# Attention scores on TensorE: the low parts of the keys as 64-row matmuls, two heads in different row groups

## The chip, the cores and the metric

One Trainium2 chip, of which the kernel uses one core. The metric is the device time of one execution in microseconds. Before the change three executions took 2203.68, 2203.01 and 2199.96 us, with a median of 2203.01 us.

## The reference, cut to what matters

The reference is one layer of a hybrid encoder block on 512 frames of width 2048: RMSNorm, one wide input projection, sixteen heads of banded softmax attention beside four heads of gated linear attention, an output projection, a gated MLP with a short convolution, a per-layer embedding gate, and a last norm. The change lies in the attention scores:

```python
def one_chunk(args):
    c, qc = args
    start = c * CHUNK
    kb = lax.dynamic_slice_in_dim(k_pad, start, band, axis=1)
    vb = lax.dynamic_slice_in_dim(v_pad, start, band, axis=1)
    s = jnp.einsum('bqhd,bkhd->bhqk', qc, kb).astype(jnp.float32) * scale + bias
    valid = (start + key_off) >= 0
    s = jnp.where(valid[None, None, None, :], s, neg)
    pr = jax.nn.softmax(s, axis=-1).astype(vb.dtype)
    return jnp.einsum('bhqk,bkhd->bqhd', pr, vb)
```

The head dimension is 64. All operands are float32.

## The kernel before, in words

Nearly all the work is on TensorE (PE). Each float32 operand of a large matmul is split into a high part, which is the value rounded to the faster matmul type fp32r, and a low part, the remainder. A product is then three matmuls: high by high, high by low, low by high. The weights are split while the kernel runs: ScalarE (ACT) writes the high part of a weight page and VectorE (DVE) subtracts it to get the low part (tile `w`). The large projections use seven products in place of eight (operands named `R11`, `N1`, `T3` and so on), and one product of one output block is one step: 24 matmuls of 128x128 by 128x256 into one of the PSUM banks `accA`, `accB`, `accC`. ACT and DVE collect the banks into a page `u`.

The order of the work is written out by hand. The main loop goes through the steps, and an `agenda` tells for each step which further pieces are issued before or after its product. A helper class (line 64, under which nearly every instruction is recorded) keeps the instructions of PE, ACT and DVE in program order.

The attention belongs to eight units of the first stage, one unit for two heads (s = 0 and 1). `attend` hangs its pieces on the agenda, from two to thirteen steps behind the unit's start. `high` and `low` make the operands from `u`, whose partitions 0 to 63 hold head 0 and 64 to 127 hold head 1:

- `Q` of a head holds the high part of its 64 query rows in the head's own half of the partitions, and the low part in the other half.
- `Kh` holds the keys' high part in both halves, and `Kl` the keys' low part in both halves.

A matmul of all 128 rows of `Q` with `Kh` is therefore (query high + query low) by key high, and one with `Kl` is (query high + query low) by key low. `scores(h)` issues both into the PSUM tile `psc` of a head, of which there are four rotating banks for `psc` and for the transposed probabilities `ptr`. `TILES` puts the four query tiles into three parts, h = 0, 1 and 2, with rows of 512, of 384, and twice of 256 key columns. `scores` of one unit is thus 16 matmuls, 8 of them with `Kl`. One step later `soft` on DVE reads `psc` (output `sc` or `scb`), ACT takes the exponential, PE turns the result (`ptr`), ACT evicts it (`PT`), and `values` multiplies with `V` (output `py`). The matmuls of `py` have 64 output columns, and the two heads write to different halves of the PSUM partitions.

Of the kernel before, what the change touches and what calls it, by code (L numbers as in the profile page):

```python
# [8 lines left out]
F32 = mybir.dt.float32  # L9
# [3 lines left out]
ALU = mybir.AluOpType  # L13

P = 128
# [27 lines left out]
def encoder_block(ctx: ExitStack, tc: tile.TileContext, A, out):  # L43
# [26 lines left out]
    vec, act, ten = InOrder(nc.vector), InOrder(nc.scalar), InOrder(nc.tensor)  # L70
# [49 lines left out]
    def psum_aux(name):  # L120
        return aux[0](name)
# [648 lines left out]
    TILES = ((3,), (2,), (1, 0))  # L770
# [3 lines left out]
    def attend(unit):  # L774
        b, M = unit.u, {}
        o = unit.o
# [25 lines left out]
        def low():  # L802
            for s in range(2):
                a, z = slice(s * 64, s * 64 + 64), slice(64 - s * 64, 128 - s * 64)
                vec.scalar_tensor_tensor(M["Q", s][z], o[a, 0, :], 0.125, M["Q", s][a].bitcast(F32), ALU.mult, ALU.subtract)
                for r in (a, z):
                    vec.tensor_tensor(M["Kl", s][r], o[a, 1, :], M["Kh", s][a].bitcast(F32), ALU.subtract)

        def scores(h):
            for s in range(2):  # L810
                psc = M["psc", s, h] = psum_aux("psc")
                for i, qt in enumerate(TILES[h]):
                    w = slice(256 * i, 256 * i + max(P * (qt + 1), 256))
                    nn = w.stop - w.start
                    ql = M["Q", s][:, qt * P:(qt + 1) * P]
                    ten.matmul(psc[:, w], ql, M["Kh", s][:, :nn], start=True, stop=False)
                    ten.matmul(psc[:, w], ql, M["Kl", s][:, :nn], start=False, stop=True)

        def soft(h):
            t, at = (tile_("scb", 768) if h == 1 else tile_("sc", 1024)), 0  # L820
# [43 lines left out]
        def result():  # L864
            if b % 2 == 0:
                ypair[:] = [page("c", "yp").rearrange("p (s t) -> p s t", s=2)]
            act.activation(ypair[0][:, b % 2, :], M["y"], AF.Copy)

        items = [(2, 7, load_e if b else lambda: None), (2, 2, high), (3, 1, low), (4, 1, mask), (5, 0, load_v), (11, 1, result)]
        if b % 2:  # L870
            items.append((12, 1, lambda: store_pair(mixd, b // 2, ypair[0][:, 0, :], ypair[0][:, 1, :])))
        for h in range(3):
            items += [(t + h, k, lambda f=f, h=h: f(h)) for t, k, f in (
                (5, 6, scores), (6, 1, soft), (7, 1, normal), (7, 5, turn), (8, 1, evict), (8 + (h == 1), 4, values))]
# [75 lines left out]
    for a, b in zip(stages[2:], stages[3:]):  # L950
        i0 = base[a.units[-1]]
        for n, p in enumerate(PLAIN):
            op = PRODUCTS[p][1]
            for g in range(2):
                start = 2 * n + 2 + g
                if g and b.chained:
                    start = max(start, 5)
# [878 lines left out]
```

## Time and profile before

| | |
|---|---|
| median of three executions | 2203.01 us |
| span of the profiled execution | 6266.3 us |
| matmuls in it | 18248 |
| PE busy | 6253.6 us (100%) |
| DVE busy | 1910.0 us (30%) |
| ACT busy | 1349.7 us (22%) |

The profiled execution is 2.84 times as long as the median of the executions without a profile. The two kinds of time are therefore kept apart below: "profiled" and "unprofiled". The profile has no record of the granted clock (its column PEclk shows 1.00 throughout). The profiled execution's own time is its span, 6266.3 us; what lies around it was not recorded.

How to read it: a row of grouped instructions gives the engine, the operation, output<-inputs, the shape, the count after x, then the busy time in us and the mean duration of one in ns, and after the last bar the idle time of the engine before them with what ended it. PE's matmul rows overlap one another, so the busy time over the count, not the mean, is the distance from one to the next. The chain of waits is followed back from the last instruction.

### The profile page before, as it was taken

Reading aid. Unit: us, or ns where it says so; the run is one execution under the profiler, and the core shown is the slowest. Engines: PE = TensorE matmul, PEld = TensorE weight load, DVE = VectorE, ACT = ScalarE, POOL = GpSimd, SP = SyncE. Lnnn points to the kernel's source line nnn. Section 1 sums busy time; section 2 is a strip of 40 time slices with the busy share of each in tenths; the row PEclk is TensorE's granted clock in tenths of the full one; section 3 lists DMA queues with packets and bytes.
Section 4 is the critical chain, followed back from the end, with each engine's and each line's share of the span. In section 5 each row is a group of like instructions: output and inputs, shape, how many; then the busy total and the mean of one; then the engine's idle time right before and its main releaser. Section 6 shows DMA issues by size and latency. Waiting matters only on the chain.

```text
span 6266.3 us, 45637 instructions
## 1 busy us (share of the span) xinstructions
PE 6253.6 (100%) x18248; PEld 5819.7 (93%) x18248; DVE 1910.0 (30%) x2585; ACT 1349.7 (22%) x1960; POOL 215.6 (3%) x261
## 2 busy tenths in 40 slices
PE   9999999999999999999999999999999999999999
PEld 5555999988989799999999999999999999999999
DVE  2222222222222233333333333333333232233333
ACT  2111111222221222222222222222222121222322
POOL 0000000000000000000000000000000000000000
DMA  1123222222222334344444443333333242333432
GB/s 67 34 81 64 61 71 57 72 74 63 70 70 87 110 100 122 101 108 116 113 113 103 112 107 92 83 78 87 79 108 95 61 113 70 109 101 114 121 110 88
DMA packets 200037, 561.39 MB, mean 90 GB/s; under 512 B 21808, under 2 KB 64048, under 8 KB 199824
## 3 DMA queue, kind: packets, MB, share of 16 engines
q1 hardware_dynamic: 163184, 431.28, 21.0%
q0 software_dynamic: 34656, 124.27, 11.5%
q8 instruction: 143, 2.34, 0.2%
q10 hardware_dynamic: 1984, 2.92, 0.1%
q14 instruction: 70, 0.57, 0.0%
HBM read 484.99 MB, written 119.54 MB: 96 GB/s over the span
## 4 chain that ended last, share of the span: by engine, by line
PE 100%; DVE 0%; issue 0%; DVEq 0%; ACT 0%; POOL 0%; POOLq 0%
PE accA L64 48%; PE accC L64 24%; PE accB L64 12%; PE v L64 5%; PE vaA L64 2%; PE vaC L64 1%; PE pp L64 1%; PE psc L64 1%; PE ptr L64 1%; PE py L64 1%; PE po L64 1%; PE vaD L64 1%; PE vaB L64 1%; PE plr L64 0%; PE pu L64 0%; PE pat L64 0%
## 5 line engine op out<-in xcount | busy, mean ns | idle before, releaser
L64 PE MATMUL accA<-h,w 128*128 128x256 f32 x5088 | 1695.5, 563 | 0.0
L64 PEld LDWEIGHTS accA<-h,w 128*128 128x128 f32 x5088 | 1673.7, 473 | 13.1 <-issue 11.6
L64 PE MATMUL accC<-h,w 128*128 128x256 f32 x4248 | 1347.7, 542 | 0.0
L64 PEld LDWEIGHTS accC<-h,w 128*128 128x128 f32 x4248 | 1330.8, 454 | 1.6 <-issue 0.6
L64 DVE TENSOR_TENSOR w<-s,w 128x1024 fp32r<-128x1024 f32 (+1 forms) x381 | 458.4, 1203 | 1100.4 <-ACT w L64 1100.4
L64 DVE TENSOR_TENSOR w<-l,w 128x1024 fp32r<-128x1024 f32 (+1 forms) x320 | 383.2, 1197 | 612.1 <-ACT w L64 607.6
L64 ACT ACTIVATE u<-accA 128x256 f32<-128x256 f32 x302 | 116.1, 384 | 2033.4 <-PE accA L64 2033.4
L64 ACT ACTIVATE w<-l 128x1024 fp32r<-128x1024 f32 (+1 forms) x320 | 331.8, 1037 | 956.1 <-PE accC L64 557.4
L64 ACT ACTIVATE w<-s 128x1024 fp32r<-128x1024 f32 (+1 forms) x381 | 395.0, 1037 | 327.5 <-PE accB L64 203.2
L64 PE MATMUL accA<-up_R,w 128*128 128x256 f32 x1056 | 325.3, 531 | 0.0
L64 PE MATMUL accA<-up_N,w 128*128 128x256 f32 x1056 | 324.2, 530 | 0.0
L64 PE MATMUL accB<-up_R,w 128*128 128x256 f32 x1056 | 323.7, 529 | 0.0
L64 PEld LDWEIGHTS accA<-up_R,w 128*128 128x128 f32 x1056 | 320.5, 441 | 1.6 <-issue 0.8
L64 PEld LDWEIGHTS accA<-up_N,w 128*128 128x128 f32 x1056 | 320.6, 442 | 0.0
L64 PEld LDWEIGHTS accB<-up_R,w 128*128 128x128 f32 x1056 | 320.5, 442 | 0.0
L64 PE MATMUL v<-w,h 128*128 128x512 f32 x384 | 318.6, 1100 | 0.0
L64 PEld LDWEIGHTS v<-w,h 128*128 128x128 f32 x384 | 165.2, 431 | 150.5 <-issue 150.1
L64 DVE TENSOR_TENSOR s<-s,l 128x1024 f32<-128x1024 f32 (+1 forms) x176 | 211.2, 1200 | 0.0
L64 DVE TENSOR_TENSOR u<-u,accC 128x256 f32<-128x256 f32 x102 | 43.0, 421 | 547.7 <-PE accC L64 547.7
L64 DVE TENSOR_TENSOR u<-u,accA 128x256 f32<-128x256 f32 x98 | 41.3, 421 | 510.4 <-PE accA L64 510.4
L64 DVE TENSOR_TENSOR u<-u,accB 128x256 f32<-128x256 f32 x100 | 42.1, 421 | 479.4 <-PE accB L64 479.4
L64 ACT ACTIVATE u<-accC 128x256 f32<-128x256 f32 x98 | 37.7, 384 | 603.5 <-PE accC L64 603.5
(303 smaller groups left out, 5554.9 us busy)
## 6 DMA issues: line engine op xcount, KB each, us to landing
l<-in_w_up SPq DMA_DIRECT2D x132, 512.0 KB, 3.5
s<-in_w_up SPq DMA_DIRECT2D x84, 512.0 KB, 3.5
s<-in_w_up POOLq DMA_DIRECT2D x84, 512.0 KB, 5.5
l<-in_w_dn SPq DMA_DIRECT2D x56, 448.0 KB, 3.4
l<-in_w_blk SPq DMA_DIRECT2D x48, 512.0 KB, 3.5
s<-in_w_blk SPq DMA_DIRECT2D x32, 512.0 KB, 3.5
s<-in_w_blk POOLq DMA_DIRECT2D x32, 512.0 KB, 6.1
l<-in_w_out SPq DMA_DIRECT2D x28, 512.0 KB, 3.6
```

The costliest lines, as they stand in the source:

```text
L64: ins = f(*args, **kw)
```

## The change

`low` writes the keys' low part only in the head's own half of the partitions, which removes one of two DVE instructions per head. `scores` multiplies `Kl` with only the 64 rows that hold the query's high part, so the product of the two low parts falls away. The order is also another one: both heads' PSUM tiles are taken first, and for each query tile there follow `Kh` of head 0, `Kh` of head 1, `Kl` of head 0 (rows 0 to 63), `Kl` of head 1 (rows 64 to 127).

```diff
@@ attend: low, scores
             for s in range(2):
                 a, z = slice(s * 64, s * 64 + 64), slice(64 - s * 64, 128 - s * 64)
                 vec.scalar_tensor_tensor(M["Q", s][z], o[a, 0, :], 0.125, M["Q", s][a].bitcast(F32), ALU.mult, ALU.subtract)
-                for r in (a, z):
-                    vec.tensor_tensor(M["Kl", s][r], o[a, 1, :], M["Kh", s][a].bitcast(F32), ALU.subtract)
+                vec.tensor_tensor(M["Kl", s][a], o[a, 1, :], M["Kh", s][a].bitcast(F32), ALU.subtract)
 
         def scores(h):
             for s in range(2):
-                psc = M["psc", s, h] = psum_aux("psc")
-                for i, qt in enumerate(TILES[h]):
-                    w = slice(256 * i, 256 * i + max(P * (qt + 1), 256))
-                    nn = w.stop - w.start
-                    ql = M["Q", s][:, qt * P:(qt + 1) * P]
-                    ten.matmul(psc[:, w], ql, M["Kh", s][:, :nn], start=True, stop=False)
-                    ten.matmul(psc[:, w], ql, M["Kl", s][:, :nn], start=False, stop=True)
+                M["psc", s, h] = psum_aux("psc")
+            for i, qt in enumerate(TILES[h]):
+                n = max(P * (qt + 1), 256)
+                for name in ("Kh", "Kl"):
+                    for s in range(2):
+                        rows = slice(0, P) if name == "Kh" else slice(s * 64, s * 64 + 64)
+                        ten.matmul(M["psc", s, h][:, 256 * i:256 * i + n], M["Q", s][rows, qt * P:(qt + 1) * P],
+                                   M[name, s][rows, :n], start=name == "Kh", stop=name == "Kl")
```

On TensorE, at the first attention unit and h = 0 and 1 (`_3107` and `_3108` are the high parts of head 0 and head 1, `_3109` and `_3110` the low parts, `_3105` and `_3106` the queries; `accB`, `accA` and `accC` are products of the input projection):

```order
 L64 MATMUL psc<-Kh_3107,Q_3105 128x512
+L64 MATMUL psc<-Kh_3108,Q_3106 128x512
 L64 MATMUL psc<-Kl_3109,Q_3105 128x512
-L64 MATMUL psc<-Kh_3108,Q_3106 128x512
 L64 MATMUL psc<-Kl_3110,Q_3106 128x512
 L64 MATMUL accA<-h_102,w 128x256 x24
 L64 MATMUL psc<-Kh_3107,Q_3105 128x384
+L64 MATMUL psc<-Kh_3108,Q_3106 128x384
 L64 MATMUL psc<-Kl_3109,Q_3105 128x384
-L64 MATMUL psc<-Kh_3108,Q_3106 128x384
 L64 MATMUL psc<-Kl_3110,Q_3106 128x384
```

Head 1's high product moves ahead of head 0's low product, and the two low products stand one behind the other; the number of matmuls is the same, and the shape shown is the output's, so that the 64 rows of the low products can't be seen in it.

On DVE, in `low` of the same unit (`u` is the unit's output, the `w` behind it the low part of a weight page that a coming product needs):

```order
 L64 SCALAR_TENSOR_TENSOR Q_3105<-u,Q_3105 64x512
-L64 TENSOR_TENSOR Kl_3109<-u,Kh_3107 64x512 x2
+L64 TENSOR_TENSOR Kl_3109<-u,Kh_3107 64x512
 L64 SCALAR_TENSOR_TENSOR Q_3106<-u,Q_3106 64x512
-L64 TENSOR_TENSOR Kl_3110<-u,Kh_3108 64x512 x2
+L64 TENSOR_TENSOR Kl_3110<-u,Kh_3108 64x512
 L64 TENSOR_TENSOR w<-l_2938,w 128x1024
```

Two of six instructions are gone ahead of the weight's low part, in each of the eight units; nothing else moves on this engine. ACT and POOL keep their instructions and their order. On SP's DMA queue one store of the attention's result (`mix_R`<-`yp`) stands two places later, behind the loads of a weight page and of a page for the MLP; all else stands as it did.

## The prediction

> **What bounds the kernel now.** I read the page first, then the groups of instructions by form, the busy time by stretches, and at last the order of time around the scores. The page's head, its engines and its chain of waits:
>
> ```profile
> span 6266.3 us, 45637 instructions
> PE 6253.6 (100%) x18248; PEld 5819.7 (93%) x18248; DVE 1910.0 (30%) x2585; ACT 1349.7 (22%) x1960; POOL 215.6 (3%) x261
> PE 100%; DVE 0%; issue 0%; DVEq 0%; ACT 0%; POOL 0%; POOLq 0%
> ```
>
> The reader is to see that in the profiled execution PE is the whole chain: nobody makes it wait. But this execution is 2.84 times as long as the unprofiled median (6266.3 / 2203.01), so the question is what of this picture holds at the true speed. The groups of the attention's stretch (1100 to 1900 us), of a later one (3100 to 4200 us) and of the whole tell which durations change with the stage:
>
> ```profile
> L64 PE MATMUL accC<-in_R,w 128*128 128x256 f32 x216 | 91.8, 689 | 0.0
> ```
>
> ```profile
> L64 DVE TENSOR_TENSOR s<-s,l 128x1024 f32<-128x1024 f32 x18 | 21.9, 1215 | 0.0
> ```
>
> ```profile
> L64 PE MATMUL accC<-h,w 128*128 128x256 f32 x1056 | 324.7, 530 | 0.0
> ```
>
> ```profile
> L64 DVE TENSOR_TENSOR s<-s,l 128x1024 f32<-128x1024 f32 x152 | 185.1, 1218 | 0.0
> ```
>
> In the attention's stretch a 256-column matmul takes 91.8 / 216 = 425 ns, later 324.7 / 1056 = 307 ns; the unprofiled execution has 2203.01 us for 18248 matmuls, 121 ns for each if PE does nothing else. The groups by form show that nearly all of these have 256 columns, so a column costs at most about 0.47 ns unprofiled, against 1.66 profiled here. The DVE instruction of 1024 columns takes 1.22 us there and in the mean of the whole. So PE was slowed in the profile, DVE was not, and unprofiled DVE is a much larger share: 1910.0 of 2203 us, 87%. By stretches:
>
> ```profile
> 1100.00:1900.00 800.00, 800.00 (x2054) 724.34 (x2054) 214.41 (x503) 176.88 (x332) 27.27 (x31) 1.00 0.27 71
> 3100.00:4200.00 1100.00, 1100.00 (x3697) 1100.00 (x3696) 378.79 (x443) 233.91 (x311) 55.91 (x64) 1.00 0.40 99
> ```
>
> (Columns: stretch, length, then busy time and count of PE, weight loads, DVE, ACT, POOL, the clock, and DMA.) In the attention's stretch 800 us of PE shrink to 800 x 0.47 / 1.66 = 227 us, while DVE keeps its 214 us. Unprofiled, the two engines are near balance there; either can be the bound, and that is the heart of this prediction.
>
> **The change, step by step.** First the low products. Their groups, and the first unit's scores in order of time:
>
> ```profile
> L64 PE MATMUL psc<-Kl,Q 128*128 128x256 f32 x32 | 22.1, 691 | 0.0
> ...
> L64 PE MATMUL psc<-Kl,Q 128*128 128x512 f32 x16 | 17.3, 1079 | 0.0
> ...
> L64 PE MATMUL psc<-Kl,Q 128*128 128x384 f32 x16 | 13.7, 859 | 0.0
> ```
>
> ```profile
> 1170.69 1.00 PE L64 MATMUL psc<-Kh,Q 128*128 128x512 f32 x1
> 1171.53 1.00 PE L64 MATMUL psc<-Kl,Q 128*128 128x512 f32 x1
> 1172.21 1.15 PE L64 MATMUL psc<-Kh,Q 128*128 128x512 f32 x1
> 1173.05 1.16 PE L64 MATMUL psc<-Kl,Q 128*128 128x512 f32 x1
> 1173.89 6.46 PE L64 MATMUL accA<-h,w 128*128 128x256 f32 x15
> ```
>
> From start to start a 512-column matmul takes 0.84 us (once 0.68), 1.64 ns a column. The 64 low products stream 32x256 + 16x512 + 16x384 = 22528 columns: 36.9 us profiled. If the two heads' 64-row matmuls run side by side, half goes: 18.5 us profiled, and 22528 x 0.47 / 2 = 5.3 us unprofiled. No row shows two row groups at once. The nearest shows two column groups: `py` ahead of a transpose, both of 128 columns of float32.
>
> ```profile
> 1208.81 3.94 PE L64 MATMUL accA<-h,w 128*128 128x256 f32 x9
> 1212.68 3.43 PE L64 MATMUL py<-PT,va 128*64 128x128 f32 x16
> 1216.04 2.01 PE L64 MATMUL ptr<-ident,scb 128*128 128x128 f32 x5
> ```
>
> Sixteen `py` take 1216.04 - 1212.68 = 3.36 us, 0.21 each, where five `ptr` take about 0.40 each: the halves do run in pairs. I take full overlap from this row; the other end is none, no gain.
>
> The same rows price the switch between matmuls of the whole array and of a part. Nine `accA` should take 9 x 0.42 = 3.78 us and take 3.87: the first `py` comes 0.09 us late. The sixteen `py` take just eight slots of 0.42, so leaving them costs 0 here. The weight loads of the same place show why a switch could cost more:
>
> ```profile
> 1209.23 3.01 PEld L64 LDWEIGHTS accA<-h,w 128*128 128x128 f32 x7
> 1212.68 2.57 PEld L64 LDWEIGHTS py<-PT,va 128*64 128x64 f32 x16 [0.43 <-issue]
> 1216.04 1.73 PEld L64 LDWEIGHTS ptr<-ident,scb 128*128 128x128 f32 x6 [0.79 <-issue]
> ```
>
> In a stream the loads run without a break; at a switch they sit idle for 0.43 or 0.79 us and start only with their own matmul. The change makes 64 switches: each pair of `Kl` is entered and left, 4 pairs in each of 8 units. Bounds: 0, and 64 x 0.09 = 5.8 us, profiled. Unprofiled, if the 0.09 follows the array's speed it is 0.09 x 0.47 / 1.66 = 0.025 us, 1.6 us in all; if it is a fixed delay, 5.8 us. I take the middle, 3.5 us (0.055 a switch).
>
> Here the Trainium skill speaks against the change: "TensorEngine Tiling (Array Packing)", Key Properties, says that a change of the tiling mode, not just of the tile, drains TensorE. The idle weight loads above agree that nothing is loaded ahead. "TensorE: Matmul & The Clock Gate", Single matmul latency, gives a lone warm matmul 398 cycles at 2.4 GHz beyond its columns, an estimated 0.166 us for one drain; 64 of them would be 10.6 us, and the sum below would end at 2206.1 us instead of 2199.0. The row's 0.09 us on the slower array is about half of that, so I weigh it as a rival.
>
> Second, the DVE instructions:
>
> ```profile
> 1141.88 0.69 DVE L64 SCALAR_TENSOR_TENSOR Q<-u,Q 64x512 fp32r<-64x512 f32 x1
> 1142.58 1.38 DVE L64 TENSOR_TENSOR Kl<-u,Kh 64x512 fp32r<-64x512 f32 x2
> 1143.98 0.69 DVE L64 SCALAR_TENSOR_TENSOR Q<-u,Q 64x512 fp32r<-64x512 f32 x1
> 1144.68 1.39 DVE L64 TENSOR_TENSOR Kl<-u,Kh 64x512 fp32r<-64x512 f32 x2
> 1146.10 1.22 DVE L64 TENSOR_TENSOR w<-l,w 128x1024 fp32r<-128x1024 f32 x1
> ```
>
> Two `Kl` take 1.40 us, so one of each two removes 0.70 us, 16 times: 11.2 us of DVE. Profiled this is worth nothing, since PE never waits for DVE; PE's slow stream covers it. Unprofiled the cover is 227 us of PE over 214 us of DVE, and the `w` behind these instructions is what PE's coming product waits for. Bounds: 0 (PE stays the bound) and -11.2 us (DVE is). I take a fifth, 2.2 us: the chain of waits in the attention's stretch shows DVE idle until another engine's work ends, so on these rows it is not yet the bound:
>
> ```profile
> DVE w L64 <- ACT w L64: 148.0, 18, 14.0
> ...
> DVE sc L64 <- PE psc L64: 119.3, 26, 14.1
> ```
>
> Third, the order. Head 0's `psc` is now complete three slots after the start instead of two, head 1's after three instead of four. DVE, which waits for `psc` (the last row), gets head 0 a slot later, at most 512 x 0.47 = 0.24 us, 24 times, if it stands ready; ACT's exponentials queue behind it. This is one reason for a fifth and no more. Head 1's bank must be free one matmul earlier; with four banks in rotation I cost that at nothing, and if it were not, PE's whole queue would stand behind that matmul for up to 0.24 us. The store that SP issues two places later is read only by the next stage: nothing; if that were late, the next stage's first load would be.
>
> The sum, profiled: 6266.3 - 18.5 + 5.8 = 6253.6 us. Unprofiled, against the median: 2203.0 - 5.3 + 3.5 - 2.2 = 2199.0 us, 0.18% less. Changes under about 0.2% (4.4 us) can't be told from none on this kernel, whose three runs lie 0.17% apart.
>
> **The rivals.**
>
> - DVE is the bound in the attention's stretch. For it: 214 of 227 us before any gaps. Against it: the two waits above, which are DVE waiting. Then PE's part is hidden and all of the DVE work counts: 2203.0 - 11.2 = 2191.8 us.
> - The switches are dear, and the kernel is slower. Place: ahead of and behind each pair of `Kl`. On a faster array the weight load at a switch is no longer hidden by the matmul ahead. The shortest load of `py` took 132 ns, so a switch may cost 0.09 + 0.13 = 0.22 us, 64 x 0.22 = 14.1 us: 2203.0 - 5.3 + 14.1 = 2211.8 us, with PE bound and DVE's relief worth nothing. It decides from 5.3 / 64 = 0.08 us a switch, and is over 0.2% from 0.15 us. The skill's drain of 0.166 us would lie there. Against it: `py` is entered 16 times with no more than the 0.09.
>
> ```profile
> L64 PEld LDWEIGHTS py<-PT,va x320: 132/294/294, 1212.7 to 1878.1; 128*64 128x64 f32 x160
> ```
>
> - The row groups don't run side by side, so the change doesn't do what it says: 2203.0 + 3.5 - 2.2 = 2204.3 us. For it: no row shows row groups. Against it: the pairs of `py`.
>
> **How the numbers follow.** My forecast, with pairs side by side, switches of 0.025 to 0.09 us and little from DVE, has 0.49 and runs from 2195 to 2203; I predict its 2199.0. DVE as the bound has 0.19 (2191 to 2195), dear switches 0.16 (2206 to 2212), no overlap 0.16 (2202 to 2207). The range of 2191 to 2208 leaves out the far end of the dear switches and whatever goes beyond the DVE work. Faster by over 0.2%, below 2198.6: a little under half of the forecast and all of the DVE case, 0.41. Slower by over 0.2%, above 2207.4: most of the dear switches and a rest of the third rival, 0.15. Within: 0.44.
>
> **What would show it.** In the profile after, the low products' starts come in pairs, and the second of a pair starts within some hundredths of a us of the first; the scores of h = 0 take about 2.5 us instead of 3.2. The next `accA` starts no more than 0.1 us late. `Kl` on DVE counts 16 instead of 32. The profiled span falls by about 13 us. If it falls so and the unprofiled time doesn't, the cover by DVE or a fixed cost of the switches is the cause. The prediction is wrong if the starts within a pair are a full matmul apart, if weight loads stand idle for much more than the 0.43 us at each switch, or if the unprofiled time falls by more than the 7.5 us that PE's and DVE's shares here make without the switches.

## The result, and the profile after

The changed kernel is slower. Eighteen executions have a median of 2210.13 us (2204.35 to 2213.88), eighteen of the kernel before, the three from ahead of the change among them, 2203.35 us (2199.22 to 2211.17). The ratio is 1.0028, with a 95% interval of 1.0020 to 1.0035: 6.2 us, or 4.4 to 7.7. The ratio isn't the plain quotient of the two medians, which lie 6.8 us apart; here and in the experiments the quotient lies within the interval, and the differences given are the ratio's. I had forecast a gain, to 2199.0 us, and the range ended at 2208.

The profile of the changed kernel, its head, engines and chain of waits:

```profile
span 2208.3 us, 45621 instructions
PE 2188.7 (99%) x18248; PEld 2128.6 (96%) x18248; DVE 1865.6 (84%) x2569; ACT 1322.4 (60%) x1960; POOL 215.0 (10%) x261
PE 82%; DVE 7%; DMA 6%; ACT 2%; issue 2%; POOL 0%; SPq 0%; DVEq 0%; ACTq 0%; POOLq 0%
```

This profile ran at the array's full speed (granted clock 0.998), the first profile of before did not. So I ran the kernel before once more for its trace (2205.49 us), and all readings from here on compare these two. Its head:

> The kernel before, unedited, to have its trace at the array's full speed. The switch theory: the first unit's scores of 512 columns take four slots of about 0.225 us with no gap behind them, about 0.21 us less than the changed kernel's, whose weight loads wait twice; py, which is entered and left 16 times, shows the same waits of about 0.2 us. The order theory (head 0's scores come too late for DVE): DVE waits for psc less here than the 3.3 us of the changed kernel.

```profile
span 2203.8 us, 45637 instructions
PE 2181.5 (99%) x18248; PEld 2131.3 (97%) x18248; DVE 1874.0 (85%) x2585; ACT 1321.4 (60%) x1960; POOL 215.3 (10%) x261
PE 85%; DVE 6%; DMA 5%; ACT 2%; issue 2%; POOL 0%; ACTq 0%; DVEq 0%; SPq 0%; POOLq 0%
```

The reader is to see that DVE is busy 85% of the time, as the prediction worked out from the slow profile, and that PE still holds most of the chain. One visit of the scores, the same unit at h = 0, in order of time (start, length, engine, group), first before:

```profile
434.78 0.40 PE L64 MATMUL psc<-Kh,Q 128*128 128x512 f32 x1
435.01 0.40 PE L64 MATMUL psc<-Kl,Q 128*128 128x512 f32 x1
435.25 0.39 PE L64 MATMUL psc<-Kh,Q 128*128 128x512 f32 x1
435.48 0.40 PE L64 MATMUL psc<-Kl,Q 128*128 128x512 f32 x1
435.72 1.30 PE L64 MATMUL accA<-h,w 128*128 128x256 f32 x10
```

and in the changed kernel, the matmuls and then the weight loads:

```profile
435.92 0.63 PE L64 MATMUL psc<-Kh,Q 128*128 128x512 f32 x2
436.48 0.51 PE L64 MATMUL psc<-Kl,Q 64*128 64x512 f32 x2
436.92 1.30 PE L64 MATMUL accA<-h,w 128*128 128x256 f32 x9
```

```profile
435.81 0.31 PEld L64 LDWEIGHTS psc<-Kh,Q 128*128 128x128 f32 x2
436.48 0.19 PEld L64 LDWEIGHTS psc<-Kl,Q 64*128 64x128 f32 x2 [0.37 <-issue]
436.92 1.22 PEld L64 LDWEIGHTS accA<-h,w 128*128 128x128 f32 x10 [0.25 <-issue]
```

Two low products take 0.51 us together, in the trace 3 ns from start to start: the row groups do run side by side. But the visit isn't shorter. Before, four matmuls take 435.72 - 434.78 = 0.94 us, 0.235 each. After, three slots should take 0.71; they take 436.92 - 435.92 = 1.00 us, and in the 1.30 us that follow there is room for nine `accA` instead of ten, 0.11 us more. That is 0.40 us too much for two switches, 0.20 each. The weight loads show where: at each switch they stand idle (0.37 and 0.25 us) and start only together with their own matmul, while in an unbroken stream the next load runs beside the matmul ahead. In this trace a load of the stream starts 0.11 us ahead of its matmul (the median); at all 64 switches it is 2 ns or less. A switch costs time in two places: the matmul behind it starts 0.09 us late (0.327 us behind a `Kh` of 512 columns, where a slot is 0.236), and the slot behind that one is 0.11 us too long (0.22 us for 256 columns of `accA`, where a slot is 0.113).

Added up over all 24 visits, from the matmul ahead of the first `Kh` to the third behind the last `Kl`, the trace has 29.5 us before and 37.1 us after. The side-by-side matmuls save 8 x 0.236 + 8 x 0.174 + 16 x 0.114 = 5.1 us (slots of 512, 384 and 256 columns), so 64 switches cost 37.1 - 29.5 + 5.1 = 12.7 us, 0.198 us each. The 7.6 us by which the visits differ lie within the interval of the result. Nothing was shown by this alone about DVE's relief and about the new order; the experiments take them apart.

### The profile page after: what moved, and what is told of

The parts are those of the page before. It is cut to its first block, busy times and chain, and to the rows that moved or that the text cites. A ratio compares the mean times of both kernels' runs of the same rounds, so it can differ in the third digit from the quotient of the medians.

```text
span 2208.3 us, 45621 instructions
## 1 busy us (share of the span) xinstructions
PE 2188.7 (99%) x18248; PEld 2128.6 (96%) x18248; DVE 1865.6 (84%) x2569; ACT 1322.4 (60%) x1960; POOL 215.0 (10%) x261
## 4 chain that ended last, share of the span: by engine, by line
PE 82%; DVE 7%; DMA 6%; ACT 2%; issue 2%; POOL 0%; SPq 0%; DVEq 0%; ACTq 0%; POOLq 0%
PE accA L64 41%; PE accC L64 21%; PE accB L64 10%; PE v L64 4%; DVE w L64 2%; DVE h L64 1%; PE psc L64 1%; PE py L64 1%; ACT w L64 1%; DMA s<-in_w_up 1%; DMA s<-in_w_blk 1%; PE ptr L64 1%; DVE u L64 1%; PE vaA L64 1%; DMA wva_P_r<-in_w_v_a 1%
## 5 line engine op out<-in xcount | busy, mean ns | idle before, releaser
L64 PE MATMUL accA<-h,w 128*128 128x256 f32 x5088 | 615.0, 278 | 0.8 <-DVE w L64 0.4
L64 PEld LDWEIGHTS accA<-h,w 128*128 128x128 f32 x5088 | 594.8, 188 | 4.6 <-issue 2.3
L64 PE MATMUL accC<-h,w 128*128 128x256 f32 x4248 | 510.4, 277 | 0.0
L64 PEld LDWEIGHTS accC<-h,w 128*128 128x128 f32 x4248 | 495.0, 188 | 0.7 <-issue 0.2
L64 PE MATMUL accA<-up_N,w 128*128 128x256 f32 x1056 | 126.9, 277 | 0.5 <-ACT u L64 0.5
L64 PE MATMUL accA<-up_R,w 128*128 128x256 f32 x1056 | 127.1, 277 | 0.0
L64 PEld LDWEIGHTS accA<-up_N,w 128*128 128x128 f32 x1056 | 123.0, 188 | 0.7 <-ACT u L64 0.7
L64 PEld LDWEIGHTS accA<-up_R,w 128*128 128x128 f32 x1056 | 123.0, 188 | 0.5 <-issue 0.5
L64 PEld LDWEIGHTS accB<-up_R,w 128*128 128x128 f32 x1056 | 123.1, 188 | 0.0
L64 PE MATMUL v<-w,h 128*128 128x512 f32 x384 | 88.9, 392 | 0.3 <-ACT h L171 0.3
```

The lines of the kernel that those rows point to most:

```text
L64: ins = f(*args, **kw)
```

## The experiments

My theory was that the switches alone cost the time. The rivals were the new order (head 0's scores come later, DVE waits), a cost of each 64-row pair wherever it stands, two row groups that hinder each other, and DVE as the bound.

**The order alone**: 128 rows and both DVE instructions again, the changed order kept.

```diff
-                vec.tensor_tensor(M["Kl", s][a], o[a, 1, :], M["Kh", s][a].bitcast(F32), ALU.subtract)
+                for r in (a, z):
+                    vec.tensor_tensor(M["Kl", s][r], o[a, 1, :], M["Kh", s][a].bitcast(F32), ALU.subtract)
...
-                        rows = slice(0, P) if name == "Kh" else slice(s * 64, s * 64 + 64)
+                        rows = slice(0, P)
```

> The changed order with 128-row matmuls for the low parts and both DVE instructions: the order alone, no switches. The switch theory: as before, 2202 to 2205. The order theory: as the changed kernel or worse, since DVE's relief is missing, 2209 to 2214.

Measured: 2202.73 us against 2202.32, ratio 1.0002 (0.9992 to 1.0013). The order costs nothing; that rival falls. Its sign did appear in the changed kernel's trace, where DVE waits 3.3 us for `psc` and in the trace of before not at all; but with the order alone it waits 0.3 us, and with the 64-row matmuls in the old order (below) 11.0 us. So the wait goes with the longer scores, not with their order.

**DVE's second instruction put back** into the changed kernel: the first hunk above, alone.

> The changed kernel with the second DVE instruction per head put back (its result is not read): 16 instructions, 11.2 us of DVE. The switch theory has DVE's relief hiding a part of the switches' cost (64 x 0.215 - 5.2 = 8.6 us against 6.2 us measured), so putting it back costs 1 to 4 us over the changed kernel, 2211 to 2214. If DVE is the bound around the scores: about 11 us more, 2221. If DVE's relief is worth nothing: 2210.

Measured: 2210.59 us, ratio to before 1.0032 (1.0019 to 1.0046), where the changed kernel has 1.0028. The relief of 11.2 us of DVE is worth 0.9 us with an interval of about 3 us around it: nothing that can be told from zero.

**DVE's relief alone**, on the kernel before: one `Kl` tile per head kept for all units, its other half set to zero once.

```diff
             for n in ("Q", "Kh", "Kl"):
                 for s in range(2):
+                    if n == "Kl" and s in kept:
+                        M[n, s] = kept[s]
+                        continue
                     M[n, s] = tile_(f"{n}{s}", T + 64, F32R)[:, 16:16 + T] if n == "Q" else tile_(f"{n}{s}", T, F32R)
+                    if n == "Kl":
+                        kept[s] = M[n, s]
+                        nc.gpsimd.memset(kept[s][64 - s * 64:128 - s * 64].bitcast(F32), 0.0)
...
-                for r in (a, z):
-                    vec.tensor_tensor(M["Kl", s][r], o[a, 1, :], M["Kh", s][a].bitcast(F32), ALU.subtract)
+                vec.tensor_tensor(M["Kl", s][a], o[a, 1, :], M["Kh", s][a].bitcast(F32), ALU.subtract)
```

> The kernel before with one Kl tile per head kept for all units, its other half set to zero once on POOL, so that DVE writes one half only: 128-row matmuls, the order of before, no low by low product, DVE relieved by 11.2 us. The switch theory: no switches, so only DVE's relief shows, 1 to 4 us below the kernel before, 2199 to 2202. If DVE is the bound there: 2192. If its relief is worth nothing: 2203.

Measured: 2204.19 us, ratio 1.0006 (0.9996 to 1.0015). Again nothing, from the other side. I had expected 1 to 4 us here; that part of my theory fell. The stretch of the attention (330 to 550 us; columns as in the prediction), of the kernel before and then with the zeroed half, shows how little a busy share says:

```profile
330.00:550.00 220.00, 219.14 (x1976) 211.44 (x1975) 198.42 (x492) 157.85 (x321) 24.43 (x28) 1.00 0.87 239
```

```profile
330.00:550.00 220.00, 219.49 (x1991) 212.70 (x1990) 190.06 (x479) 158.80 (x321) 24.41 (x28) 1.00 0.88 242
```

DVE was busy for 198 of 220 us, 90%, and freeing it changed nothing in the time.

**64 rows without pairs**: the order of before, so that each 64-row `Kl` stands alone between two 128-row `Kh`.

```diff
-                    ten.matmul(psc[:, w], ql, M["Kl", s][:, :nn], start=False, stop=True)
+                    r = slice(s * 64, s * 64 + 64)
+                    ten.matmul(psc[:, w], M["Q", s][r, qt * P:(qt + 1) * P], M["Kl", s][r, :nn], start=False, stop=True)
```

> The order of before, with 64-row matmuls for the low parts: each Kl stands alone between two Kh, so nothing runs side by side and there are 128 switches instead of 64 (a Kl of 64 rows is entered and left 64 times). The switch theory, by the 0.198 us that the two traces give: 2203 + 128 x 0.198 = 2228 us, 2224 to 2231. A rival, that two row groups side by side hinder each other: no side by side here, so about the time of before, 2203 to 2206.

Measured: 2229.4 us, ratio 1.0119 (1.0104 to 1.0134), 26.2 us. The visits add up to 54.0 us in its trace: 24.5 us for 128 switches, 0.191 each. One visit of 512 columns:

```profile
443.40 0.40 PE L64 MATMUL psc<-Kh,Q 128*128 128x512 f32 x1
443.73 0.50 PE L64 MATMUL psc<-Kl,Q 64*128 64x512 f32 x1
444.16 0.51 PE L64 MATMUL psc<-Kh,Q 128*128 128x512 f32 x1
444.59 0.50 PE L64 MATMUL psc<-Kl,Q 64*128 64x512 f32 x1
445.02 1.19 PE L64 MATMUL accA<-h,w 128*128 128x256 f32 x8
```

Slots of 0.43 instead of 0.235 us, with nothing beside them: the row groups don't hinder each other, the alternation costs. A single 64-row matmul shows 0.50 us, as the pair together showed 0.51.

**Each pair twice**: the changed kernel with the pair of `Kl` issued a second time behind the first (the low part is added twice).

```diff
-                for name in ("Kh", "Kl"):
+                for k, name in enumerate(("Kh", "Kl", "Kl")):
...
-                                   M[name, s][rows, :n], start=name == "Kh", stop=name == "Kl")
+                                   M[name, s][rows, :n], start=k == 0, stop=k == 2)
```

> The changed kernel with each pair of 64-row Kl matmuls issued twice, the second behind the first (the low part is added twice): 64 switches as changed, but twice the 64-row pairs. The switch theory: only the columns count, 11264 x 0.45 = 5.1 us over the changed kernel, 2213 to 2217. The rival, that each 64-row pair carries its own fixed cost: 64 x 0.198 + 5.1 = 17.8 us more, 2228.

Measured: 2214.84 us, ratio 1.0053 (1.0040 to 1.0065), 11.7 us over before and so 5.5 over the changed kernel. In its trace four 64-row matmuls follow each other without a gap, 440.13 - 439.47 = 0.66 us where two took 0.44:

```profile
438.91 0.63 PE L64 MATMUL psc<-Kh,Q 128*128 128x512 f32 x2
439.47 0.73 PE L64 MATMUL psc<-Kl,Q 64*128 64x512 f32 x4
440.13 1.63 PE L64 MATMUL accA<-h,w 128*128 128x256 f32 x12
```

A further pair costs its columns only, 0.22 us. The fixed cost belongs to the change from 128 to 64 rows and back, not to the pair.

**Fewer switches**: the two query tiles of h = 2 taken together, 48 switches instead of 64 (the accumulation flags follow: one start per bank).

```diff
-            for i, qt in enumerate(TILES[h]):
-                n = max(P * (qt + 1), 256)
-                for name in ("Kh", "Kl"):
+            last = len(TILES[h]) - 1
+            for name in ("Kh", "Kl"):
+                for i, qt in enumerate(TILES[h]):
+                    n = max(P * (qt + 1), 256)
...
-                                   M[name, s][rows, :n], start=name == "Kh", stop=name == "Kl")
+                                   M[name, s][rows, :n], start=name == "Kh" and i == 0, stop=name == "Kl" and i == last,
+                                   **({"skip_group_check": True} if last else {}))
```

> The changed kernel with the two query tiles of h = 2 taken together: four Kh, then the four Kl, so 48 switches instead of 64, all else as changed. The switch theory: 16 x 0.198 = 3.2 us less than the changed kernel, 2205 to 2208. The rival, that each pair of 64-row matmuls costs its 0.4 us wherever it stands: no difference, 2210.

Measured: 2209.46 us, ratio 1.0021 (1.0010 to 1.0032), 4.6 us over before instead of 6.2. In time this is inconclusive, since the interval holds both expectations. In the trace the visits take 34.4 us, 2.7 less than in the changed kernel (3.2 expected), and still 4.9 more than before.

**What PE's time is worth here**: the kernel before without its 64 `Kl` matmuls, so that the scores lack the keys' low parts.

```diff
-                    ten.matmul(psc[:, w], ql, M["Kh", s][:, :nn], start=True, stop=False)
-                    ten.matmul(psc[:, w], ql, M["Kl", s][:, :nn], start=False, stop=True)
+                    ten.matmul(psc[:, w], ql, M["Kh", s][:, :nn], start=True, stop=True)
```

> The kernel before without its 64 Kl matmuls (the scores lack the keys' low parts), DVE's instructions all kept: what PE's time is worth around the scores. If PE is the bound: 22528 columns at 0.45 ns, 10 us less, 2192 to 2195. If DVE, busy for 198 of 220 us there, is the bound: 2200 to 2203.

Measured: 2201.73 us against 2205.08, ratio 0.9988 (0.9977 to 1.0000), 2.6 us less. The visits are 9.4 us shorter in the trace (20.2 of 29.5), so three quarters of the relief don't arrive. Then the same without the 32 DVE instructions that make `Kl`:

```diff
-                for r in (a, z):
-                    vec.tensor_tensor(M["Kl", s][r], o[a, 1, :], M["Kh", s][a].bitcast(F32), ALU.subtract)
```

> The kernel before without its 64 Kl matmuls and without the 32 DVE instructions that make Kl (the scores lack the keys' low parts): about 10 us of PE and 22 us of DVE less. If PE and DVE are both near the bound around the scores, so that relief of one turns into waiting for the other: now PE's 10 us show, 2192 to 2196. If a third engine or the transfers set the pace there: as without the matmuls alone, 2200 to 2203.

Measured: 2206.39 us against 2204.18, ratio 1.0012 (1.0001 to 1.0023). I had expected 2192 to 2196, and this expectation failed outright: with both engines relieved nothing is gained. So neither is the bound in the sense of my prediction. The traces show where the time comes back. One place is the attention itself (320 to 560 us): there PE waits 0.7 us in all in the kernel before, 5.0 us without the low keys, and 3.9 us without their DVE work too. The longest of these waits, before and then without the low keys (who waited for whom: us in total, times, longest):

```profile
PE ptr L64 <- DVE sc L64: 0.4, 1, 0.4
PE accA L64 <- ACT u L64: 0.3, 1, 0.3
```

```profile
PE ptr L64 <- DVE sc L64: 2.6, 2, 1.7
PE accA L64 <- ACT u L64: 1.5, 2, 1.1
```

From the first `psc` to the last `py` it takes 203.6 us before, 199.4 without the low keys and 200.7 without both: of 9.4 and 8.3 us of relief in the visits, 4.2 and 3.0 arrive. The other place lies right behind the attention: the matmuls `pp` of the embedding, which need a loaded and split input `ps`. In order of time (the bracket is the idle time before, and who ended it), of the kernel before, then without the low keys, then without their DVE work too:

```profile
583.74 0.49 PE L64 MATMUL pp<-ps,w 128*128 128x512 f32 x1 [0.52 <-ACT ps L64]
585.00 22.01 PE L64 MATMUL pp<-ps,w 128*128 128x512 f32 x95 [0.77 <-DVE ps L64]
```

```profile
583.34 0.50 PE L64 MATMUL pp<-ps,w 128*128 128x512 f32 x1 [2.35 <-ACT ps L64]
584.60 23.44 PE L64 MATMUL pp<-ps,w 128*128 128x512 f32 x95 [0.76 <-DVE ps L64]
```

```profile
580.21 0.50 PE L64 MATMUL pp<-ps,w 128*128 128x512 f32 x1 [2.02 <-ACT ps L64]
581.47 23.60 PE L64 MATMUL pp<-ps,w 128*128 128x512 f32 x95 [0.76 <-DVE ps L64]
```

The two relieved kernels wait 1.5 to 1.8 us longer for `ps`, and take 1.4 to 1.6 us longer over `pp`. The second is the clock: in both traces the granted clock fell to 0.50 for 3.4 us just there, and a matmul of 512 columns took 0.43 us in that time instead of 0.23. The stretch of 580 to 590 us in the same order (the clock is the third number from the end; 0.83 is the mean of 1.00 and of 0.50 for 3.4 us):

```profile
580.00:590.00 10.00, 8.72 (x52) 7.37 (x51) 9.78 (x13) 7.65 (x12) 0.76 (x1) 1.00 1.02 404
```

```profile
580.00:590.00 10.00, 6.89 (x27) 5.32 (x26) 9.43 (x13) 6.64 (x10) 0.28 (x1) 0.83 1.00 388
```

```profile
580.00:590.00 10.00, 9.03 (x31) 7.07 (x32) 6.30 (x9) 5.51 (x9) 1.26 (x2) 0.83 1.03 402
```

From the first `psc` to the end of `pp` it is 274.0 us before, 274.9 and 274.5 without the low keys: nothing of the relief is left. The zeroed half reads the same way: its last `py` comes 1.7 us earlier than before, it waits 0.95 us for `ps` instead of 0.52, and its `pp` takes 23.61 us at the same drop of the clock. Arriving early isn't the condition of the drop: fewer switches and each pair twice, which arrive later than the kernel before, have it too. The five traces with it waited 0.95 to 2.76 us for the first `ps`, the five others at full speed 0.52 us or less. That this idle time brings the drop on is a guess from these ten traces; no run tests it.

Why `ps` comes late isn't shown either. The transfers are full in this stretch (545 to 610 us, DMA share 1.00 in the kernel before), which would fit, but it is argued from this row alone:

```profile
545.00:610.00 65.00, 63.72 (x461) 59.31 (x460) 45.44 (x59) 39.61 (x58) 6.77 (x9) 1.00 1.00 359
```

These are single traces, and single executions of the kernel before lie up to 12 us apart (2199.22 to 2211.17).

No version that keeps the keys' low parts beats the kernel before: the zeroed half and the order alone equal it within 0.15%.

## Why the prediction was wrong

- **Pairs side by side: right.** I took the pairs of `py` as the nearest row; the low products start 3 ns apart and save 5.1 us of PE against the 5.3 worked out.
- **The switches: the step that failed.** I took 0.055 us each, 3.5 us in all, from bounds of 0 and 0.09 us. They cost 0.198 us each, 12.7 us. The bounds came from one visit of `py`, in a profile whose array ran at about a quarter of the speed, 425 ns for 256 columns where it is 113 ns at full speed, and I read that visit wrongly. Leaving isn't free in it: the last pair of `py` starts 0.67 us ahead of `ptr`, where a slot is 0.42. It looked free because the slot behind the entrance took 0.17 us instead of 0.42 and made up for it. And 0.09 us isn't the most: `py` is entered 0.24 us late in seven of the sixteen visits of the slow profile, the second visit among them (0.66 us from `accA` to `py`, where a slot is 0.42):

```profile
1215.37 0.74 PE L64 MATMUL py<-PT,va 128*64 128x128 f32 x2
1216.04 0.49 PE L64 MATMUL ptr<-ident,scb 128*128 128x128 f32 x1
```

```profile
1239.95 0.73 PE L64 MATMUL accA<-h,w 128*128 128x256 f32 x1
1240.61 0.49 PE L64 MATMUL py<-PT,va 128*64 128x128 f32 x2
```

  So on the slow array the slot behind a switch gave back what the switch took. At full speed it takes nearly the same, 0.16 us behind the entrance of `py`, but a slot is only 0.109 us there, and so it adds to the cost. I had scaled the price down with the array or kept it; the part that the long slots covered had no place in my bounds. At full speed the same visit of `py` shows it:

```profile
344.84 1.41 PE L64 MATMUL accA<-h,w 128*128 128x256 f32 x11
346.18 1.09 PE L64 MATMUL py<-PT,va 128*64 128x128 f32 x16
347.20 0.87 PE L64 MATMUL ptr<-ident,scb 128*128 128x128 f32 x6
```

  Eleven `accA` at 0.113 are 1.24 us and take 1.34; eight pairs at 0.109, the distance of two pairs in the stream, are 0.87 us and take 1.02. That is 0.25 us for two switches, where the slow profile had 0.09. The loads that start only with their own matmul were the sign in the slow profile, and I gave them no price. Their idle time alone is no sign, and a stream is not always without a break: in the same profile the loads of the 512-column scores idle for 0.34 to 0.39 us with no switch near.
- **The rival of dear switches was the right one**, with 0.22 us each against 0.198 measured, and 2211.8 us against 2210.13. Its mechanism was right, a load at the switch that nothing hides; its sum was near by luck, 0.09 us and a load of 0.13, where the trace has 0.09 us ahead of the matmul and 0.11 in the slot behind it. I gave it a chance of 0.16 because `py` showed no more than 0.09, which was the same misread visit. The Trainium skill spoke on its side: "TensorEngine Tiling (Array Packing)", Key Properties, has a change of tiling mode drain TensorE, and the traces agree in that no load starts ahead of its matmul at any of the switches. That the array is empty by then they don't show: by the profile's modelled ends the first low product above starts at 436.48 us, 0.07 us before the last `Kh` ends. The drain estimated from "TensorE: Matmul & The Clock Gate", Single matmul latency, 0.166 us, lay nearer to the measured 0.198 than my own term. That section speaks of a lone bf16 matmul and not of a switch, so the nearness may be chance.
- **DVE's relief: a fifth of 11.2 us was too much.** The zeroed half gains at most 0.9 us (the lower end of its interval), and the instruction put back can't tell its 0.9 us from zero, nor from my 2.2. My two waits (DVE idle for ACT and PE) were the right reading; the 214 of 227 us, 198 of 220 at full speed, were no sign of a bound.
- **The order and the store on SP: nothing**, as costed. The order alone measures 1.0002; the store stands two places later in the zeroed half too, which measures 1.0006.
- **The sum by the measured terms**: 2203.0 - 5.1 + 12.7 + 0 = 2210.6 us, against 2210.13. Of the signs that I had named, the starts in pairs came true; the next `accA` comes 0.29 us late (1.00 us against 0.71) instead of 0.1 at most.

## What to carry to other kernels

Two half-height matmuls side by side pay only where many of them stand in a row: here a change from whole-array to half-array matmuls and back costs 0.4 us, and one pair saves 0.11 to 0.24 us. By these figures two pairs of 512 columns in a row would gain a little (an estimate, 0.47 against 0.40 us); no run here has a version that gains. Group by mode first, then count the switches against the columns. And price a fixed delay from a trace taken at the speed at which the kernel is timed, and from all its visits: on the slowed array here the slot behind a switch gave back what the switch took.

## What the runs showed of the hardware that I had not expected

An added cost on PE came through nearly in full (7.6 us in the trace, 6.2 measured; 24.5 and 26.2; 13.2 and 11.7), while a relief of 9.4 us on the same place came through with 2.6, and of PE and DVE together with nothing. In five of the ten traces at full speed the granted clock fell to 0.50 once behind the attention, for 3.4 us, and `pp` took 1.3 to 1.6 us longer than in the kernel before. A profile can have an array nearly four times slower than at full speed (425 ns against 113 in the attention) and still show 1.00 in its clock column when it holds no record of the clock.
